# One plain pair of weight tiles instead of two at the start of the second feed-forward block

## The chip, the cores and the metric

The kernel runs on one NeuronCore of a Trainium2 chip. The metric is the device time of one execution in microseconds (us), lower is better. TensorE (PE) multiplies, VectorE (DVE) and ScalarE (ACT) do the elementwise work, GpSimd (POOL) a few small steps, and SyncE (SP) issues the loads. Each of them works through its own instructions in the order in which they stand.

## The reference

One encoder layer on 512 rows of 1024 features: a feed-forward block, a mixer (convolution and a two-way mLSTM), and a second feed-forward block, each between two norms and added to the residual. What the change touches is the feed-forward block:

```python
def rmsnorm(x, g):
    y = x32 * lax.rsqrt(jnp.mean(x32 * x32, axis=-1, keepdims=True) + EPS)
    return (y * g.astype(jnp.float32)).astype(x.dtype)

def swiglu(x, w_in, w_out):
    gate, up = jnp.split(x @ w_in, 2, axis=-1)
    return (jax.nn.silu(gate) * up) @ w_out
...
h = swiglu(rmsnorm(x, norm_ffn2_pre[l]), w_ffn2_in[l], w_ffn2_out[l])
x = x + FFN_RESIDUAL_SCALE * rmsnorm(h, norm_ffn2_post[l])
```

`w_ffn2_in` is 1024 x 5632 (2816 gate columns, then 2816 up columns) and `w_ffn2_out` 2816 x 1024.

## The kernel before, in words

**Precision.** Every float32 operand of a large matmul is split into a high and a low part (`split`: a copy on ACT makes the high part, a subtraction on DVE the low one, L220 and L221), and three matmuls (high x high, high x low, low x high) stand for one.

**The input product of a feed-forward block** (`ffn`). The 2816 gate and up columns are 22 pairs of 128-column weight tiles. The 512 rows are four row tiles of 128. They are handled as two row halves of 256: half 0 is row tiles 0 and 1, half 1 is row tiles 2 and 3. The 1024 features are two halves as well, so that the input is four blocks.

- *The plain way* (`plain`, L361 to L370): a weight tile against one row half is 8 k-blocks x 3 = 24 matmuls of 256 columns. A pair over both halves is 96. The first loop (L373) does row half 0 of all its weight tiles, the second (L377) does row half 1.
- *The seven products* (L398 to L419): gate and up over the two feature halves make a 2x2 block matrix of weights, the input is a 2x2 block matrix too, and seven products of 12 matmuls with added and subtracted blocks replace the eight. A pair is 84 matmuls. `w_pair` makes the weight combinations on DVE and ACT, and the pair's results are put together on DVE and ACT (L403 to L417): `x` is a PSUM tile into which products 1, 6, 7 and 4 accumulate, and it is copied out after product 1 (L403) and after product 6 (L409).
- *Combinations of the input* (`combine_x`, L272 to L293): products 5, 6, 7 and 4 need four combined blocks `t1`, `t2`, `t3`, `t4`, four subtractions (L279) and four splits, which need all four row tiles.

**Why there are plain pairs.** Row tile 3 of the second block comes last: the mixer's output product (L911) ends with it, then `post_norm` (L310) and `pre_norm` (L295) work on it with ACT, DVE and POOL in turn (sum of squares L241, a power on POOL L234, scaling L322, sum of squares, power, scaling L300), then `flip_q` (L261) transposes it on PE (L265), splits it into row half 1, and copies it for `combine_x` (L270). While that goes on, PE does row half 0 of the plain pairs. The dictionary `between` says ahead of which part of which weight tile the transposes of row tile 3 are written: `(3, 2)` is before the low-part matmuls of the fourth weight tile.

**Order.** Instructions are written in program order and a list scheduler of the framework then places them on the engines; what it made is shown below in rows of the built program. Weights come through four raw buffers (`rawp`); `w_get` splits a given number of tiles ahead.

Of the kernel before, what the change touches and what calls it, by code (L numbers as in the profile page):

```python
# [20 lines left out]
KD = D // P  # L21
# [8 lines left out]
WARM = 24  # L30
WARM2 = 4
ON_POOL = (0, 1)
PLAIN = 2


@with_exitstack
def encoder_kernel(ctx: ExitStack, tc: tile.TileContext, a: dict, out: bass.AP):
# [22 lines left out]
    def ps():  # L60
        return psum.tile([P, 512], F32, tag="ps", name=nm("ps"))
# [13 lines left out]
    def blk(i, n=P):  # L75
        return slice(i * n, (i + 1) * n)

    def ch(v):
        return v.rearrange("p (c t) -> p c t", t=P)


    w1i, w1o = a["w_ffn1_in"][0], a["w_ffn1_out"][0]
# [5 lines left out]
    def cols(w, c0):  # L88
        return w[:, c0:c0 + P].rearrange("(k p) f -> p k f", p=P), KD

    def rows(w, r0):
        return w[r0:r0 + P, :], 1

    def one(v):
        return [v[0]], v[1]

    stream = []
    for w_in, w_out in ((w1i, w1o), (w2i, w2o)):
        if w_in is w2i:
            stream += [cols(wm, c) for c in (Q0, Q0 + P, K0, K0 + P)]  # L100
            stream += [cols(wm, O0 + i * P) for i in range(4)]
            stream += [cols(wm, CG)]
            stream += [(wm[blk(i, 2 * P), V0:V0 + 512].rearrange("(k p) f -> p k f", p=P), 2) for i in range(4)]
            for i in range(4):
                stream += [cols(wm, c + i * P) for c in ((CG, HC, BG) if i else (HC, BG))]
            stream += [rows(wo, k * P) for k in MIXK[:5]]
        for j in range(NF):
            pair = [cols(w_in, j * P), cols(w_in, DFF + j * P)]
            stream += pair if j < PLAIN else [([v[0] for v in pair], KD)]
        stream += [rows(w_out, k * P) for k in range(NF)]  # L110
    stream = [v if isinstance(v[0], list) else one(v) for v in stream]
    loaded, ready = [], []
# [67 lines left out]
    def w_get(ahead=2):  # L180
        w_split(max(0, 1 + ahead - len(ready)))
        return ready.pop(0)
# [78 lines left out]
    def flip_q(tb, xs, xq, halves=(0, 1)):  # L261
        for b in halves:
            pt = ps()
            for k in range(4):
                nc.tensor.transpose(out=pt[:, blk(k)], in_=xs[:, blk(4 * b + k)], identity=ident)  # L265
            hi, lo = xq_hl(xq, (b, tb // 2))
            split(hi[:, :, blk(tb % 2)], lo[:, :, blk(tb % 2)], ch(pt))
            if b not in xq["f"]:
                xq["f"][b] = bigt()
            nc.scalar.copy(xq["f"][b][:, :, blk(tb)], ch(pt))  # L270
# [39 lines left out]
    def post_norm(tb, acc, g, mul, after=None):  # L310
        t = [t2() for _ in range(2)]

        def weigh(i):
            nc.vector.tensor_tensor(out=t[i], in0=acc[i], in1=g[:, blk(i, 512)], op=ALU.mult)

        s0 = sumsq(acc[0])
        weigh(0)
        r = rstd([s0, sumsq(acc[1])], D, mul)
        weigh(1)
        for i in range(2):  # L320
            h = blk(i, 512)
            nc.vector.scalar_tensor_tensor(out=x_t[tb][:, h], in0=t[i], scalar=r, in1=x_t[tb][:, h], op0=ALU.mult, op1=ALU.add)  # L322
            if after:
                after(tb, h)
# [22 lines left out]
                nc.tensor.matmul(o, ww[:, k, :], x[xx][:, k, :], start=first and n == 0, stop=n == 11, skip_group_check=True)  # L347
                n += 1

    def ffn(xq, between, finish, mid=None, within=None):  # L350

        h = [bigt() for _ in range((NF + 3) // 4)]

        def act(j, pg, pu):
            sg = t2()
            nc.scalar.activation(sg, pg, AF.Silu)
            nc.vector.tensor_tensor(out=h[j // 4][:, j % 4, 0:512], in0=pu, in1=sg, op=ALU.mult)

        def plain(o, w, th, hooks=None, i=None):  # L361
            hi, lo = w
            n = 0
            for ww, xx in ((hi, 0), (hi, 1), (lo, 0)):
                if hooks and (i, n // KD) in hooks:
                    hooks[i, n // KD]()
                for k in range(KD):
                    nc.tensor.matmul(  # L368
                        o, ww[:, k, :], xq_hl(xq, (k // 4, th))[xx][:, k % 4, :], start=n == 0, stop=n == 3 * KD - 1)
                    n += 1  # L370

        ws, pts = [], []
        for i in range(2 * PLAIN):  # L373
            ws.append(w_get(min(2, 3 - i) if i < 3 else 1))
            pts.append(ps())
            plain(pts[i][:, 0:256], ws[i], 0, between, i)
        for i in range(2 * PLAIN):  # L377
            plain(pts[i][:, 256:512], ws[i], 1)
            if i == 0:
                combine_x(xq)  # L380
            if i % 2:
                act(i // 2, pts[i - 1], pts[i])

        h0, h1 = slice(0, 256), slice(256, 512)
        right = {1: (0, 0), 2: (1, 0), 3: (1, 1), 4: "t4", 5: "t1", 6: "t2", 7: "t3"}

        def product(n, w, o, first):
            mm_part(o[:, h0], w[n], xq_hl(xq, right[n]), first)  # L390

        def last(j, w, x, c, u):
            product(4, w, x, False)
            hj = h[j // 4][:, j % 4, :]
            nc.vector.tensor_tensor(out=hj[:, h0], in0=x[:, h0], in1=c[:, h0], op=ALU.mult)

        pending = None
        for j in range(PLAIN, NF):  # L398
            w = w_get(1 if j < NF - 1 else 2)
            x, y, z = ps(), ps(), ps()  # L400
            a_, u, c = t2(), t2(), t2()
            product(1, w, x, True)
            nc.scalar.copy(a_[:, h0], x[:, h0])  # L403
            product(5, w, y, True)
            nc.scalar.copy(u[:, h0], y[:, h0])
            if pending:
                last(*pending)
            product(6, w, x, False)
            nc.scalar.copy(a_[:, h1], x[:, h0])  # L409
            product(3, w, y, False)  # L410
            nc.vector.tensor_tensor(out=c[:, h1], in0=y[:, h0], in1=a_[:, h1], op=ALU.add)
            product(2, w, z, True)
            nc.vector.tensor_tensor(out=c[:, h0], in0=z[:, h0], in1=a_[:, h0], op=ALU.add)
            nc.scalar.activation(c, c, AF.Silu)
            product(7, w, x, False)
            nc.vector.tensor_tensor(out=u[:, h1], in0=x[:, h0], in1=u[:, h0], op=ALU.add)
            nc.vector.tensor_tensor(out=h[j // 4][:, j % 4, h1], in0=u[:, h1], in1=c[:, h1], op=ALU.mult)  # L417
            pending = (j, w, x, c, u)
        last(*pending)  # L419

        acc = [[ps(), ps()] for _ in range(NT)]
        hs = None
        ks = {}

        def mm_out(tb, half, k, hT, w):
            for hh, ww in ((0, 0), (0, 1), (1, 0)):
                nc.tensor.matmul(  # L427
                    acc[tb][half], hT[hh][:, blk(tb)], w[ww][:, blk(half, 512)],
                    start=(k == 0 and hh == 0 and ww == 0), stop=(k == NF - 1 and hh == 1),
                )  # L430

        for k in range(NF):
            if k % 2 == 0:
                hs = bigt(F32R)
            hT = (hs[:, 2 * (k % 2), 0:512], hs[:, 2 * (k % 2) + 1, 0:512])
            split(hT[0], hT[1], h[k // 4][:, k % 4, 0:512])
            ks[k] = (hT, w_get(2 if k < NF - TAIL else min(2, NF - 1 - k)))
            if k == 12 and mid:
                mid()
            if k < NF - TAIL:  # L440
                for tb in range(NT):
                    for half in range(2):
                        mm_out(tb, half, k, *ks[k])
        for tb in range(NT):
            todo = [(half, k) for half in range(2) for k in range(NF - TAIL, NF)]
            if tb == NT - 1 and mid:
                todo.sort(key=lambda v: v[1])
            for n, (half, k) in enumerate(todo):
                if n == 4 and within:
                    within(tb)  # L450
                mm_out(tb, half, k, *ks[k])
            finish(tb, acc[tb])


    xT1 = new_xq()
    xs = [pre_norm(tb, g_pre) for tb in range(2)]
# [7 lines left out]
    st1 = {}  # L464

    def rest1(tb):
        st1[tb] = pre_norm(tb, g_pre)
# [63 lines left out]
        if tb >= 2:  # L531
            flip(tb - 2, st[tb - 2], st["xT"])

    ffn(xT1, {(1, 0): lambda: rest1(2), (1, 1): lambda: rest1(3), (2, 0): lambda: flip_q(2, st1[2], xT1), (2, 2): lambda: flip_q(3, st1[3], xT1)}, finish1, wgates, within1)
    xT = st["xT"]


# [363 lines left out]
    xT3 = new_xq()  # L901
    xs = {}
    for tb in range(NT):
        acc = [ps(), ps()]
# [14 lines left out]
    g_post3 = gain("norm_ffn2_post")  # L919
# [1 line left out]
    def store(tb, h):  # L921
        nc.sync.dma_start(out[0, blk(tb), h], x_t[tb][:, h])

    ffn(xT3, {(3, 2): lambda: flip_q(3, xs[3], xT3)}, lambda tb, acc: post_norm(tb, acc, g_post3, 4.0, store))


_INS = [
# [26 lines left out]
```

## Time and profile before

| | us |
|---|---|
| three runs | 934.29 (median), 932.46, 934.36 |
| the profiled execution: time | 933.59 |
| the profiled execution: span from first to last instruction | 931.9 |
| PE busy | 920.1 (99%) |
| DVE busy | 633.5 (68%) |
| ACT busy | 417.7 (45%) |

The page also shows the mean granted TensorE clock, 0.996 of full speed. Times in the views are us from the start of the span. The difference of 1.7 between time and span lies around the instructions.

The second block starts at about 581 us. Its input product lasts to about 813 us and its output product to about 926 us.

### The profile page before, as it was taken

How to read it: one execution, taken by the hardware profiler on the slowest of the kernel's cores; microseconds unless marked ns; L12 is line 12 of the kernel's file. 1: busy time of each engine (PE TensorE's matmuls, PEld its weight loads, DVE VectorE, ACT ScalarE, POOL GpSimd, SP SyncE). 2: the span in 40 equal slices, each digit the busy share in tenths (PEclk: the TensorE clock that was granted, in tenths of full speed). 3: DMA queues.
4: the chain of work that ended last, by engine and by line, in shares of the span. 5: the costliest groups of instructions: out<-in, count | busy, mean ns of one | idle time of the engine just before them, and what ended most of it. 6: DMA issues, size and time to landing. Idle time of an engine off the chain costs nothing.

```text
span 931.9 us, 14877 instructions
## 1 busy us (share of the span) xinstructions
PE 920.1 (99%) x6075; PEld 834.9 (90%) x6075; DVE 633.5 (68%) x1028; ACT 417.7 (45%) x685; POOL 39.2 (4%) x64
## 2 busy tenths in 40 slices
PE   7999999999999999999999999999999999999997
PEld 6999999999888889987888888999999999888885
DVE  5989988888822248496767736888888888932223
ACT  6655554556611126452324425645545545721111
POOL 3000000000200001000011000000000000000000
PEclk9999999999999999999999999999999999999999
DMA  8434343344333313231422501323343343443202
GB/s 249 139 91 119 108 128 100 98 129 126 104 133 95 104 52 113 67 93 46 128 76 69 158 24 37 99 73 110 107 121 92 108 120 92 158 136 91 67 9 82
DMA packets 125101, 94.35 MB, mean 101 GB/s; under 512 B 4053, under 2 KB 114665, under 8 KB 125033
## 3 DMA queue, kind: packets, MB, share of 16 engines
q1 hardware_dynamic: 125032, 93.41, 33.7%
q8 instruction: 47, 0.77, 0.3%
q14 instruction: 22, 0.17, 0.1%
HBM read 91.30 MB, written 2.10 MB: 100 GB/s over the span
## 4 chain that ended last, share of the span: by engine, by line
PE 97%; issue 1%; DMA 1%; DVE 1%; ACT 0%; SPq 0%; DVEq 0%; POOLq 0%; POOL 0%; ACTq 0%
PE ps L347 42%; PE ps L427 26%; PE ps L338 13%; PE ps L911 5%; PE ps L368 4%; PE ps L765 2%; PE ps L265 1%; PE ps L832 1%; PE ps L838 1%; DMA gb<-in_norm_ffn_pre_dram 1%; PE ps L801 0%; PE ps L307 0%; PE ps L784 0%; PE ps L806 0%; PE ps L869 0%
## 5 line engine op out<-in xcount | busy, mean ns | idle before, releaser
L221 DVE TENSOR_TENSOR wlo<-raw,whi 128x1024 fp32r<-128x1024 f32 x199 | 241.3, 1220 | 143.3 <-ACT whi L220 137.9
L220 ACT CAST whi<-raw 128x1024 fp32r<-128x1024 f32 x201 | 206.2, 1050 | 222.9 <-PE ps L427 124.2
L347 PE MATMUL ps<-big,whi 128*128 128x256 f32 x1920 | 264.4, 280 | 0.0
L347 PEld LDWEIGHTS ps<-big,whi 128*128 128x128 f32 x1920 | 243.1, 188 | 0.4
L427 PE MATMUL ps<-whi,big 128*128 128x512 f32 x704 | 221.6, 395 | 0.0
L427 PEld LDWEIGHTS ps<-whi,big 128*128 128x128 f32 x704 | 132.2, 188 | 31.1
L347 PE MATMUL ps<-big,wlo 128*128 128x256 f32 x960 | 150.9, 280 | 0.0
L427 PE MATMUL ps<-wlo,big 128*128 128x512 f32 x352 | 139.0, 395 | 0.0
L347 PEld LDWEIGHTS ps<-big,wlo 128*128 128x128 f32 x960 | 129.1, 188 | 0.0
L427 PEld LDWEIGHTS ps<-wlo,big 128*128 128x128 f32 x352 | 66.1, 188 | 15.3
L338 PE MATMUL ps<-big,whi 128*128 128x512 f32 (+1 forms) x384 | 79.8, 358 | 0.0
L338 PEld LDWEIGHTS ps<-big,whi 128*128 128x128 f32 x384 | 63.4, 188 | 11.0 <-issue 0.2
L347 PE MATMUL ps<-big,ws 128*128 128x256 f32 x480 | 65.2, 280 | 0.0
L347 PEld LDWEIGHTS ps<-big,ws 128*128 128x128 f32 x480 | 60.3, 188 | 0.0
L409 ACT COPY t<-ps 128x256 f32<-128x256 f32 x40 | 14.9, 372 | 73.3 <-PE ps L347 73.2
L338 PE MATMUL ps<-big,wlo 128*128 128x512 f32 (+1 forms) x192 | 41.2, 356 | 0.0
L241 ACT ACTIVATE junk<-ps 128x512 bf16<-128x512 f32 x24 | 14.4, 598 | 57.0 <-PE ps L427 26.8
L338 PEld LDWEIGHTS ps<-big,wlo 128*128 128x128 f32 x192 | 32.2, 188 | 5.4
L234 POOL TENSOR_TENSOR rs<-rs,nhalf 128x1 f32<-128x1 f32 x24 | 13.6, 566 | 528.7 <-DVE rs L231 528.7
L368 PE MATMUL ps<-big,whi 128*128 128x256 f32 x256 | 33.5, 283 | 0.1
L221 DVE TENSOR_TENSOR big<-big,big 128x512 fp32r<-128x512 f32 (+1 forms) x48 | 33.0, 731 | 0.7 <-ACT big L220 0.7
L368 PEld LDWEIGHTS ps<-big,whi 128*128 128x128 f32 x256 | 31.6, 190 | 0.4 <-ACT big L220 0.3
(183 smaller groups left out, 937.0 us busy)
## 6 DMA issues: line engine op xcount, KB each, us to landing
raw<-in_w_ffn_in_dram SPq DMA_DIRECT2D x88, 512.0 KB, 4.6
raw<-in_w_ffn_out_dram SPq DMA_DIRECT2D x44, 512.0 KB, 3.6
raw<-in_w_mix_in_dram SPq DMA_DIRECT2D x24, 512.0 KB, 3.9
raw<-in_w_mix_out_dram SPq DMA_DIRECT2D x8, 512.0 KB, 3.6
out_dram<-x SPq DMA_DIRECT2D x8, 256.0 KB, 2.0
x<-in_x_dram SPq DMA_DIRECT2D x4, 256.0 KB, 4.3
x<-in_x_dram SPq DMA_DIRECT2D x2, 512.0 KB
gb<-in_norm_ffn_post_dram SPq DMA_DIRECT2D x2, 512.0 KB, 4.0
```

The costliest lines, as they stand in the source:

```text
L220: nc.scalar.copy(out=hi, in_=src)
L221: eng.tensor_tensor(out=lo, in0=src, in1=f32(hi), op=ALU.subtract)
L234: nc.gpsimd.tensor_tensor(out=r[:, 0:w], in0=acc, in1=nhalf[:, 0:w], op=ALU.pow)
L241: nc.scalar.activation(junk[:, 0:src.shape[1]], src, AF.Square, accum_out=s)
L265: nc.tensor.transpose(out=pt[:, blk(k)], in_=xs[:, blk(4 * b + k)], identity=ident)
L338: nc.tensor.matmul(o, ww[:, k, :], xk(xT, xx, k, sl), start=n == 0, stop=n == 3 * KD - 1)
L347: nc.tensor.matmul(o, ww[:, k, :], x[xx][:, k, :], start=first and n == 0, stop=n == 11, skip_group_check=True)
L368: nc.tensor.matmul(o, ww[:, k, :], xq_hl(xq, (k // 4, th))[xx][:, k % 4, :], start=n == 0, stop=n == 3 * KD - 1)
L409: nc.scalar.copy(a_[:, h1], x[:, h0])
L427: nc.tensor.matmul(acc[tb][half], hT[hh][:, blk(tb)], w[ww][:, blk(half, 512)], start=(k == 0 and hh == 0 and ww == 0), stop=(k == NF - 1 ...
L765: nc.tensor.matmul(pv_, xk(xT, xx, k, blk(tb)), ww[:, k % 2, :], start=n == 0, stop=n == 3 * KD - 1)
L911: nc.tensor.matmul(acc[half], yy[yi][:, k % 4, blk(tb)], wmo[k][wi][:, blk(half, 512)], start=(n == 0 and yi == 0 and wi == 0), stop=(n == ...
```

## The change

The number of plain pairs becomes a parameter of `ffn`: 2 for the first block as before, 1 for the second. The stream of weight loads follows it, the prefetch expression takes the number in, and the transposes of row tile 3 are now written before the low-part matmuls of the second weight tile, `(1, 2)`, which is the last one there is. In the second block the second pair (j = 1) is thus computed by the seven products.

```diff
-PLAIN = 2
...
-            stream += pair if j < PLAIN else [([v[0] for v in pair], KD)]
+            stream += pair if j < (2 if w_in is w1i else 1) else [([v[0] for v in pair], KD)]
...
-    def ffn(xq, between, finish, mid=None, within=None):
+    def ffn(xq, between, finish, PLAIN, mid=None, within=None):
...
-            ws.append(w_get(min(2, 3 - i) if i < 3 else 1))
+            ws.append(w_get(min(2, 2 * PLAIN - 1 - i) if i < 2 * PLAIN - 1 else 1))
...
-    ffn(xT3, {(3, 2): lambda: flip_q(3, xs[3], xT3)}, lambda tb, acc: post_norm(tb, acc, g_post3, 4.0, store))
+    ffn(xT3, {(1, 2): lambda: flip_q(3, xs[3], xT3)}, lambda tb, acc: post_norm(tb, acc, g_post3, 4.0, store), 1)
```

Line numbers after the change are one lower: L367 for L368, L346 for L347, and so on. Three places in the built programs follow. Up to the second block the five engines' rows are the same in both.

**Place A, PE, the end of row half 0 of the plain pairs.** `t_841` is row tile 3 after `pre_norm`; `big_5529` and `big_5539` hold row half 0, `big_5723` and `big_5732` row half 1. Before:

```order
L368 MATMUL ps_5902<-big_5539,whi_5824 128x256 x4
L265 MATMUL ps_5919<-ident,t_841_5758 128x128 x4
L368 MATMUL ps_5902<-big_5529,wlo_5825 128x256 x2
L265 MATMUL ps_5927<-ident,t_841_5758 128x128 x4
L368 MATMUL ps_5902<-big_5529,wlo_5825 128x256 x2
L368 MATMUL ps_5902<-big_5539,wlo_5825 128x256 x4
L347 MATMUL ps_6087<-big_5529,whi_5885 128x256 x8
L347 MATMUL ps_6087<-big_5529,wlo_5886 128x256 x4
L368 MATMUL ps_5797<-big_5723,whi_5781 128x256 x4
```

After:

```order
L367 MATMUL ps_5840<-big_5529,wlo_5788 128x256 x4
L367 MATMUL ps_5840<-big_5539,wlo_5788 128x256 x4
L264 MATMUL ps_5857<-ident,t_841_5758 128x128 x4
L264 MATMUL ps_5865<-ident,t_841_5758 128x128 x4
L346 MATMUL ps_5974<-big_5529,whi_5823 128x256 x8
L346 MATMUL ps_5974<-big_5529,wlo_5824 128x256 x4
L367 MATMUL ps_5791<-big_5723,whi_5781 128x256 x4
L367 MATMUL ps_5840<-big_5723,whi_5787 128x256 x4
```

Between the last L911 and the first L265 on `t_841` PE has 88 matmuls before and 48 after; product 1 of the first seven-product pair (L347, now L346) follows the transposes in both.

**Place B, PE, products 6, 2, 3 and 7 of the first seven-product pair.** `ps_6087` before and `ps_5974` after are its PSUM tile `x`; `big_5975` and `big_5913` hold `t2`, `big_5978` and `big_5916` `t3`. Before:

```order
L347 MATMUL ps_6087<-big_5975,whi_5894 128x256 x8
L347 MATMUL ps_6087<-big_5975,wlo_5895 128x256 x4
L347 MATMUL ps_6089<-big_5539,whi_5885 128x256 x8
L347 MATMUL ps_6089<-big_5539,wlo_5886 128x256 x4
L347 MATMUL ps_6088<-big_5732,whi_5894 128x256 x8
L347 MATMUL ps_6088<-big_5732,wlo_5895 128x256 x4
L347 MATMUL ps_6087<-big_5978,whi_5898 128x256 x8
```

After:

```order
L346 MATMUL ps_5975<-big_5732,whi_5832 128x256 x8
L346 MATMUL ps_5975<-big_5732,wlo_5833 128x256 x4
L346 MATMUL ps_5974<-big_5913,whi_5832 128x256 x4
L346 MATMUL ps_5974<-big_5913,wlo_5833 128x256 x4
L346 MATMUL ps_5974<-big_5916,whi_5836 128x256 x8
```

Before, 24 matmuls of two other products stand between the end of product 6 and product 7 into the same PSUM tile; after, none. From the end of row half 1 to the row with `wlo_5833` into `ps_5974` there are 76 matmuls of the seven-product pairs on PE after the change.

**Place C, DVE, around the first sums of squares of row tile 3** (`rs_5751` comes from them; L221 rows with `wlo` are weight splits). Before:

```order
L314 TENSOR_TENSOR t_834_5742<-ps_5674,gb_5397 128x512
L229 TENSOR_SCALAR rs_5749<-ss_5744 128x1
L221 TENSOR_TENSOR wlo_5788<-raw_5785,whi_5787 128x1024
L221 TENSOR_TENSOR wlo_5794<-raw_5791,whi_5793 128x1024
L221 TENSOR_TENSOR wlo_5825<-raw_5822,whi_5824 128x1024
L221 TENSOR_TENSOR wlo_5886<-raw_5878,whi_5885 128x1024
L221 TENSOR_TENSOR big_5723<-ps_5718,big_5723 128x4x128
L221 TENSOR_TENSOR big_5732<-ps_5727,big_5732 128x4x128
L231 SCALAR_TENSOR_TENSOR rs_5751<-ss_5747,rs_5749 128x1
```

After:

```order
L313 TENSOR_TENSOR t_834_5742<-ps_5674,gb_5397 128x512
L228 TENSOR_SCALAR rs_5749<-ss_5744 128x1
L220 TENSOR_TENSOR wlo_5788<-raw_5785,whi_5787 128x1024
L220 TENSOR_TENSOR wlo_5824<-raw_5816,whi_5823 128x1024
L220 TENSOR_TENSOR big_5723<-ps_5718,big_5723 128x4x128
L220 TENSOR_TENSOR big_5732<-ps_5727,big_5732 128x4x128
L230 SCALAR_TENSOR_TENSOR rs_5751<-ss_5747,rs_5749 128x1
```

Two weight splits fewer stand ahead; from L231 to L300 of row tile 3 the order is the same in both.

## Rows read from the trace of the kernel before

**Rows 1.** Page: busy time by engine; then the shares of the chain that ended last.

```profile
PE 920.1 (99%) x6075; PEld 834.9 (90%) x6075; DVE 633.5 (68%) x1028; ACT 417.7 (45%) x685; POOL 39.2 (4%) x64
PE 97%; issue 1%; DMA 1%; DVE 1%; ACT 0%; SPq 0%; DVEq 0%; POOLq 0%; POOL 0%; ACTq 0%
```

**Rows 2.** That chain in order of time, 581 to 800 us: start, length, what.

```profile
581.44 10.34 PE ps L368 x88
591.79 0.44 PE ps L265 x4
...
593.61 1.38 PE ps L347 x12
595.00 11.31 PE ps L368 x96
606.30 193.66 PE ps L347 x1644
```

**Rows 3.** Timeline of PE, second block's start: start, length, instruction [idle before <-releaser].

```profile
581.28 2.04 PE L368 MATMUL ps<-big,whi 128*128 128x256 f32 x16
...
586.92 2.04 PE L368 MATMUL ps<-big,whi 128*128 128x256 f32 x16
...
591.62 0.60 PE L265 MATMUL ps<-ident,t 128*128 128x128 f32 x4
...
608.52 0.63 PE L347 MATMUL ps<-big,wlo 128*128 128x256 f32 x4
```

**Rows 4.** Timeline of ACT, same stretch.

```profile
581.54 0.60 ACT L241 ACTIVATE junk<-ps 128x512 bf16<-128x512 f32 x1 [0.82 <-PE ps L911]
582.03 0.19 ACT L241 ACTIVATION_READ_ACCUMULATOR junk<-ps 128x1 f32 x1
...
609.19 0.37 ACT L409 COPY t<-ps 128x256 f32<-128x256 f32 x1 [0.52 <-PE ps L347]
```

**Rows 5.** Timeline of DVE, same stretch.

```profile
576.74 4.63 DVE L221 TENSOR_TENSOR wlo<-raw,whi 128x1024 fp32r<-128x1024 f32 x4 [0.18 <-ACT whi L220]
581.28 1.28 DVE L221 TENSOR_TENSOR big<-ps,big 128x512 fp32r<-128x512 f32 x2
582.48 0.15 DVE L231 SCALAR_TENSOR_TENSOR rs<-ss,rs 128x1 f32<-128x1 f32 x1
...
583.15 0.68 DVE L134 TENSOR_TENSOR t<-raw 128x512 f32<-128x512 f32 x1
583.75 1.41 DVE L322 SCALAR_TENSOR_TENSOR x<-t,rs,x 128x512 f32<-128x512 f32 x2
...
587.06 0.69 DVE L134 TENSOR_TENSOR raw<-raw 128x512 f32<-128x512 f32 x1
588.19 1.42 DVE L300 SCALAR_TENSOR_TENSOR t<-x,rs,gb 128x512 f32<-128x512 f32 x2 [0.44 <-POOL rs L234]
```

**Rows 6.** Timeline of POOL, same stretch.

```profile
582.77 0.55 POOL L234 TENSOR_TENSOR rs<-rs,nhalf 128x1 f32<-128x1 f32 x1 [8.96 <-DVE rs L231]
587.24 0.92 POOL L234 TENSOR_TENSOR rs<-rs,nhalf 128x1 f32<-128x1 f32 x1 [3.91 <-DVE rs L231]
```

**Rows 7.** The chain in order of time, first block's start.

```profile
24.00 0.67 DVE t L300
...
24.80 0.64 PE ps L265 x4
```

**Rows 8.** Timeline of PE, the kernel's start: two waits for a normalized row tile.

```profile
9.91 0.66 PE L265 MATMUL ps<-ident,t 128*128 128x128 f32 x4 [3.27 <-DVE t L300]
...
24.80 1.29 PE L265 MATMUL ps<-ident,t 128*128 128x128 f32 x8 [0.80 <-DVE t L300]
```

**Rows 9.** Windows: busy time and (instructions) by engine; PEclk is the column after POOL.

```profile
10.00:14.00 4.00, 4.00 (x22) 4.00 (x23) 3.35 (x6) 3.25 (x6) 1.69 (x1) 0.57 1.07 363
14.00:16.00 2.00, 1.90 (x16) 1.70 (x15) 1.18 (x2) 2.00 (x4) 1.17 (x2) 1.00 1.12 348
24.00:26.00 2.00, 1.17 (x10) 0.98 (x10) 2.00 (x3) 1.79 (x3) 0.00 (x0) 1.00 1.08 313
640.00:700.00 60.00, 60.00 (x512) 60.00 (x511) 50.33 (x80) 30.53 (x49) 0.00 (x0) 1.00 0.37 107
```

More of the change, by code (lines that the diff above doesn't have):

```diff
@@ L532, in within1 @@
             flip(tb - 2, st[tb - 2], st["xT"])
-    ffn(xT1, {(1, 0): lambda: rest1(2), (1, 1): lambda: rest1(3), (2, 0): lambda: flip_q(2, st1[2], xT1), (2, 2): lambda: flip_q(3, st1[3], xT1)}, finish1, wgates, within1)
+    ffn(xT1, {(1, 0): lambda: rest1(2), (1, 1): lambda: rest1(3), (2, 0): lambda: flip_q(2, st1[2], xT1), (2, 2): lambda: flip_q(3, st1[3], xT1)}, finish1, 2, wgates, within1)
     xT = st["xT"]
```

## Prediction

> **What bounds the kernel now.** The page comes first: PE is busy 99% of the span and holds 97% of the chain that ended last [rows 1]. So a change counts by the matmuls that it takes from PE and by the time that it leaves PE without work. The chain in order of time then shows the place of the change, 581.44 to 606.30: 88 + 2 + 6 matmuls of L368 (the short pieces stand between the transposes) for row half 0 of the four plain weight tiles, 8 transposes, 12 matmuls of L347, and 96 of L368 for row half 1, one behind the other [rows 2]. In this stretch PE waits for nothing. In the seven-product stretch 1644 matmuls take 193.66 us, 0.1178 us each, and the 96 plain ones take 11.31, again 0.1178 [rows 2]: whether PE works in the plain way or by products, its price is the count of matmuls.
>
> The plain matmuls of row half 0 are also a cover. Row tile 3 is normalized while they run, and the timelines of DVE, ACT and POOL show how long that takes: PE's last L911 is done at about 581.4, and the second half of the normalized row tile at 588.19 + 1.42 = 589.61 [rows 4, 5]. Before, its transposes came at 591.62 [rows 3], when it had been ready for two us. What cover is left afterwards decides this change.
>
> **The saving.** A pair costs 96 matmuls in the plain way and 84 by products. Before, the second block has 192 + 20 x 84 = 1872, after it 96 + 21 x 84 = 1860. Twelve fewer, at 0.1178 us: **-1.41 us**. Its cover on the other engines is dealt with below.
>
> **The first wait: transposes of row tile 3.** After the change 48 matmuls stand ahead of them (place A). The first plain matmul starts at 581.28 and the 49th at 586.92 [rows 3], so PE comes to the transposes at 586.92. Each of them is queued in PE ahead of product 1 of the first product pair, of row half 1, of everything that follows, so nothing overtakes. When is row tile 3 ready? The chain behind it starts with PE's last L911, which the change doesn't move: sum of squares at 581.54, read out by 582.03 + 0.19 = 582.22 [rows 4]. The next step, L231, comes at 582.48 since DVE is still at the two row-tile splits until then, and these stood behind four weight splits of 4.63 together, 1.16 each [rows 5]. With two of them gone (place C) L231 can follow at about 582.28, 0.2 earlier. The rest of the chain has the same order as before, so I let it keep its durations: power on POOL, L322, squares, L231, power, L300 at 588.19 [rows 5, 6], first half done after half of 1.42, at about 588.9 (the single one of rows 7 takes 0.67). From there to a transpose on PE the first block shows 24.00 + 0.67 = 24.67 to 24.80, 0.13 [rows 7]. So 588.9 + 0.13 - 0.2 = 588.82, and PE stands still from 586.92 on: **+1.9 us**. Bounds: 1.7, if the hand-over costs nothing, and 2.1, if the 0.2 is not won.
>
> The 0.2 is the doubtful part of it, for POOL has its own say. Its power takes 0.55 at 582.77 and 0.92 at 587.24 [rows 6], the second one while L134 runs on DVE from 587.06 to 587.75 [rows 5]. An earlier L231 puts the first power partly beside the L134 that stood at 583.15. The Trainium skill says in GPSIMD Engine Reference, section Specifications, that GpSimd shares its SBUF interfaces with VectorE and contends with DVE instructions that have two SBUF inputs; the trace agrees as far as these two rows go (0.92 against 0.55), and by that rule the first wait would be nearer to 2.1 than to 1.9.
>
> **The second wait.** The other half of row tile 3 is done 0.7 after the first, at 589.61 + 0.13 - 0.2 = 589.54. Four transposes take 0.44 [rows 2], so they end at 588.82 + 0.44 = 589.26: **+0.28 us**. Bounds 0.2 and 0.3.
>
> **The third wait: product 7 of the first product pair.** It accumulates into the PSUM tile that ACT has to copy out after product 6. Before, 24 matmuls (2.8 us) hide the copy; after, product 7 stands right behind (place B). The price from the same copy before: the last matmul of product 6 starts at 608.52 + 3 x 0.118 = 608.87, the next could at 608.99; the copy runs from 609.19 to 609.56 [rows 3, 4], plus 0.13: 609.69. **+0.65 us**, if ACT is free then (0.6 with a quicker hand-over, zero only if PE gets there late for another reason).
>
> **What the second product pair asks of DVE and ACT.** Between the last row-tile split and the low part of `t2` DVE has seven operations of 1.16 and four of 0.60 (four in 4.63; L134 at 583.15, the next at 583.75) [rows 5], 10.5 us together. The splits ahead of them end at about 593.1 (two weight splits from 589.4 on, then two row-tile splits of 0.6), so `t2` is complete at about 603.6. PE starts row half 1 after the transposes and product 1 at 589.54 + 0.44 + 12 x 0.118 = 591.4, ends it 48 matmuls later at 597.05, and has 76 matmuls ahead of the one that needs that low part: 606.0. Cover 2.4 us, so I put it at nothing. Without this cover PE would wait for as much as DVE is late. In the steady stretch DVE is busy 50.33 of 60 us [rows 9], so it catches up about 0.16 us per us. The weight loads are no wait: the product pair's two raw tiles are now third and fourth in the stream instead of fifth and sixth, and the gain's load, which waits for DVE's L314, has moved ahead of the third product pair's loads, first read more than 10 us later.
>
> **Sum.** -1.41 + 1.9 + 0.28 + 0.65 = +1.42 us. On the profiled execution's 933.59 that is 935.0; the median of the runs is 934.29, 0.7 higher, and I forecast from it: **935.7 us**. By the bounds of the three waits alone it is +0.5 to +1.7.
>
> **Rivals.**
>
> *The saving shows.* If row tile 3 came when PE does, PE would save 1.41 less the third wait: -0.8, 933.5. It turns from loss to gain where the three waits together stay under 1.41, so where row tile 3 is 1.4 us earlier than I reckon. For it: DVE has 2.3 us less ahead of the chain. Against it: the chain hangs on PE's last L911 at both ends, and only 0.26 us of it (582.22 to 582.48) is a wait for DVE's weight work. Even with no wait at all it would be 932.9, 0.15% less.
>
> *TensorE's clock falls.* At the start of the kernel PE idles for 3.27 us ahead of a transpose [rows 8], and in the four us from 10 on the granted clock is 0.57, then 1.00 [rows 9]; the level in between is the half speed of 1.2 GHz. That cost 4 x 0.43 = 1.7 us of full speed. After the idle 0.80 at 24 us it stays at 1.00 [rows 8, 9]. The new idle time of 1.9, and 0.28 soon after, lies between the two, nearer to the one that cost nothing. If the clock falls: +1.4 + 1.7 = +3.1, **937.4**, slower. It decides at any fall longer than a us at half speed. The Trainium skill states in TensorE: Matmul & The Clock Gate, section What's actually happening, that the gate goes back to half rate when TensorE has been idle and that activity releases it; the trace agrees for 3.27 us, and no row shows a gap like the new one.
>
> *DVE becomes the bound for the first product pairs.* The second pair's 12 or so DVE operations now run between the steps that make `t1` to `t4`, and copies on ACT stand close to the matmuls that wait for them. For it: DVE has only 16% to spare. Against it: the cover of 2.4 us. Half a weight split to a whole one late (0.6 to 1.2) would give about +2.2, 936.5.
>
> That the change does nothing is ruled out by place A.
>
> **Chances and range.** The forecast 0.58, the saving 0.12, the clock 0.17, DVE 0.13. About 0.2% (1.9 us) is what a measurement here can tell from no change; the three runs of before differ by as much. The forecast lies 0.15% up, so nearly a quarter of it, 0.13, falls over the line, with 0.16 of the clock's and 0.10 of DVE's: slower 0.39. Faster has the saving's edge and a favourable run, 0.04; the rest, 0.57, is no difference. The range goes from the saving's 933.5 to the clock case's upper end: **933.5 to 937.7**, and what it leaves out are runs beside these cases.
>
> **What would show it.** In the timeline of PE, L264 on row tile 3 with an idle time of 1.7 to 2.1 put down to DVE L299, a second of 0.2 to 0.3, and 0.6 before L346 put down to ACT L408; row half 1's 48 plain matmuls and 1764 of L346. In the timeline of DVE, L230 about 0.2 earlier against PE's last L910. Granted clock 1.00 from 586 to 600. Wrong would be: L299's end before 587; a clock under 1; waits of PE for DVE's `wlo` or combined blocks after 600 us; or a change in the output product, where I expect none.

## The result, and the profile after

The changed kernel takes 937.19 us (median of 6 runs, 936.1 to 938.37) against 934.28 (6 runs, 932.46 to 934.51): ratio 1.0035, 95% interval 1.0025 to 1.0045. It is slower by 2.9 us by the medians. The prediction's line for slower was 0.2%, and it gave "no difference" 0.57 and slower 0.39. The time lies in the predicted range; the forecast, 935.7, was too low by half of the effect.

Whole times also hold what happens before the second block, which starts anywhere between 580.5 and 582.1 us in the profiles below. So I also use the **block length**, from the start of the block's first plain matmul to the start of the kernel's last matmul, both read from the timeline of PE. Before it is 344.09 (925.38 - 581.28), after it is 346.97 (927.89 - 580.92), +2.87; the starts shown are rounded, so a last digit can be one off.

The page after (busy time; shares of the chain that ended last), as in [rows 1]:

```profile
PE 919.1 (98%) x6063; PEld 833.2 (89%) x6063; DVE 637.6 (68%) x1038; ACT 420.5 (45%) x690; POOL 39.3 (4%) x64
PE 92%; DVE 2%; DMA 2%; ACT 1%; issue 1%; SPq 0%; POOL 0%; DVEq 0%; POOLq 0%; ACTq 0%
```

PE has the 12 matmuls fewer that were reckoned (6063 for 6075). But it holds 92% of the chain instead of 97%, and loads (DMA) have 2% of it instead of 1%. Where, the chain in order of time shows, as in [rows 2] (start, length, what):

```profile
587.62 0.76 DVE t L299
588.52 0.64 PE ps L264 x4
589.18 0.63 PE ps L264 x4
589.81 1.41 PE ps L346 x12
591.22 5.66 PE ps L367 x48
596.88 9.91 PE ps L346 x84
607.24 10.30 PE ps L346 x85
...
622.00 4.92 DMA raw<-in_w_ffn_in_dram
627.55 0.69 DVE raw L133
...
632.33 4.73 DMA raw<-in_w_ffn_in_dram
637.69 0.70 DVE raw L133
...
642.22 5.17 DMA raw<-in_w_ffn_in_dram
...
649.70 152.85 PE ps L346 x1296
```

In [rows 2] nothing but PE stands between 581 and 800. Now DVE's L299 stands ahead of the transposes, as forecast, and from 622 to 647 three weight loads are on the chain, which was not. The waits of PE from 575 us on (total, times, longest), then that of DVE for loads from 590 to 815:

```profile
PE ps L264 <- DVE t L299: 1.8, 1, 1.8
PE ps L346 <- DVE t L415: 0.7, 2, 0.5
PE ps L346 <- ACT t L408: 0.5, 1, 0.5
```

```profile
DVE t L133 <- DMA raw<-in_w_ffn_in_dram: 8.5, 6, 2.3
```

Before, PE has no wait in that stretch, and DVE one for a load:

```profile
DVE t L134 <- DMA raw<-in_w_ffn_in_dram: 1.0, 1, 1.0
```

The timelines of PE, ACT, DVE and POOL at the places of [rows 3 to 6]:

```profile
580.92 2.04 PE L367 MATMUL ps<-big,whi 128*128 128x256 f32 x16
...
585.62 1.10 PE L367 MATMUL ps<-big,wlo 128*128 128x256 f32 x8
588.52 1.29 PE L264 MATMUL ps<-ident,t 128*128 128x128 f32 x8 [1.80 <-DVE t L299]
...
606.15 0.63 PE L346 MATMUL ps<-big,wlo 128*128 128x256 f32 x4
607.24 1.21 PE L346 MATMUL ps<-big,whi 128*128 128x256 f32 x8 [0.46 <-ACT t L408]
...
628.12 0.63 PE L346 MATMUL ps<-big,wlo 128*128 128x256 f32 x4
629.23 1.22 PE L346 MATMUL ps<-big,whi 128*128 128x256 f32 x8 [0.47 <-DVE t L415]
```

```profile
581.18 0.60 ACT L240 ACTIVATE junk<-ps 128x512 bf16<-128x512 f32 x1
581.67 0.19 ACT L240 ACTIVATION_READ_ACCUMULATOR junk<-ps 128x1 f32 x1
...
606.82 0.37 ACT L408 COPY t<-ps 128x256 f32<-128x256 f32 x1 [3.51 <-PE ps L346]
```

```profile
581.90 0.16 DVE L230 SCALAR_TENSOR_TENSOR rs<-ss,rs 128x1 f32<-128x1 f32 x1 [0.71 <-ACT junk L240]
...
587.62 1.41 DVE L299 SCALAR_TENSOR_TENSOR t<-x,rs,gb 128x512 f32<-128x512 f32 x2 [0.44 <-POOL rs L233]
...
620.76 2.35 DVE L220 TENSOR_TENSOR wlo<-raw,whi 128x1024 fp32r<-128x1024 f32 x2
...
626.94 0.69 DVE L133 TENSOR_TENSOR t<-raw 128x512 f32<-128x512 f32 x1 [2.29 <-DMA raw<-in_w_ffn_in_dram]
627.55 0.68 DVE L133 TENSOR_TENSOR raw<-raw 128x512 f32<-128x512 f32 x1
628.15 0.69 DVE L133 TENSOR_TENSOR raw<-raw,raw 128x512 f32<-128x512 f32 x1
628.75 0.42 DVE L415 TENSOR_TENSOR t<-ps,t 128x256 f32<-128x256 f32 x1
```

```profile
582.20 0.55 POOL L233 TENSOR_TENSOR rs<-rs,nhalf 128x1 f32<-128x1 f32 x1 [8.75 <-DVE rs L230]
586.67 0.92 POOL L233 TENSOR_TENSOR rs<-rs,nhalf 128x1 f32<-128x1 f32 x1 [3.91 <-DVE rs L230]
```

*The first three waits* are there. From the start of the 48th plain matmul (586.44) to the first transpose (588.52) it is 2.08, less the 0.12 that a matmul takes: 1.96 us lost. The third is 0.74 - 0.12 = 0.62 by the same reading, and the matmul after each wait comes 0.1 later than usual as well.

*The loads* are the new thing. Two weight splits run from 620.76 to 623.1; the first ends at about 622.0 and frees its raw buffer. The load into this buffer has landed at 626.92, and DVE stands 2.29 us at L133, which reads it. Behind L133 in DVE's row stands L415, which takes product 7's result out of the PSUM tile into which PE wants to accumulate product 4, so PE waits 0.47 us by this view and 0.75 - 0.12 = 0.63 by its starts. The same comes again near 639 (the starts are 0.23 apart, so 0.11) and at 649 (0.47 apart, so 0.35). With the 0.1 behind each, the three cost 1.4 us.

### The profile page after: what moved, and what is told of

It is laid out like the page before. It is cut to its first block, busy times and chain, and to the rows that moved or that the text cites. A ratio compares the mean times of both kernels' runs of the same rounds, so it can differ in the third digit from the quotient of the medians.

```text
span 934.4 us, 14881 instructions
## 1 busy us (share of the span) xinstructions
PE 919.1 (98%) x6063; PEld 833.2 (89%) x6063; DVE 637.6 (68%) x1038; ACT 420.5 (45%) x690; POOL 39.3 (4%) x64
## 4 chain that ended last, share of the span: by engine, by line
PE 92%; DVE 2%; DMA 2%; ACT 1%; issue 1%; SPq 0%; POOL 0%; DVEq 0%; POOLq 0%; ACTq 0%
PE ps L346 40%; PE ps L426 26%; PE ps L337 13%; PE ps L910 5%; PE ps L764 2%; PE ps L367 2%; DMA raw<-in_w_ffn_in_dram 2%; DVE wlo L220 1%; PE ps L831 1%; PE ps L837 1%; PE ps L264 1%; DMA gb<-in_norm_ffn_pre_dram 1%; PE ps L800 0%; PE ps L306 0%; DVE raw L133 0%
## 5 line engine op out<-in xcount | busy, mean ns | idle before, releaser
L346 PE MATMUL ps<-big,whi 128*128 128x256 f32 x1968 | 271.0, 280 | 1.1 <-DVE t L415 0.7
L346 PEld LDWEIGHTS ps<-big,whi 128*128 128x128 f32 x1968 | 249.0, 188 | 2.2 <-DVE t L415 1.2
L346 PE MATMUL ps<-big,wlo 128*128 128x256 f32 x984 | 154.0, 280 | 0.0
L346 PEld LDWEIGHTS ps<-big,wlo 128*128 128x128 f32 x984 | 132.1, 188 | 0.0
L337 PEld LDWEIGHTS ps<-big,whi 128*128 128x128 f32 x384 | 63.3, 188 | 11.0 <-issue 0.2
L346 PE MATMUL ps<-big,ws 128*128 128x256 f32 x492 | 68.4, 280 | 0.0
L346 PEld LDWEIGHTS ps<-big,ws 128*128 128x128 f32 x492 | 62.4, 188 | 0.0
L133 DVE TENSOR_TENSOR t<-raw 128x512 f32<-128x512 f32 x41 | 28.1, 685 | 14.2 <-DMA raw<-in_w_ffn_in_dram 14.2
L337 PEld LDWEIGHTS ps<-big,wlo 128*128 128x128 f32 x192 | 32.2, 188 | 5.4
L413 ACT ACTIVATE t<-t 128x512 f32<-128x512 f32 x41 | 25.9, 633 | 23.1 <-DVE t L410 22.3
```

The source lines that it names most:

```text
L133: nc.vector.tensor_tensor(out=o, in0=a_, in1=b_, op=op)
L337: nc.tensor.matmul(o, ww[:, k, :], xk(xT, xx, k, sl), start=n == 0, stop=n == 3 * KD - 1)
```

## The experiments

Three theories. **A**: the three early waits add up to the loss, with the 12 matmuls saved. **L**: PE's waits from 620 us on come from late weight loads (rival **V**: DVE simply has too much work there). **C**: in some executions TensorE's clock falls after the first wait. Ratios are to runs of the kernel before on the same chip, with 95% intervals.

| run | kernel | median us (before) | ratio | block length of its profile, against 344.09 |
|---|---|---|---|---|
| e1 | changed, six raw buffers | 935.99 (933.85) | 1.0024 [1.0015, 1.0033] | +3.03 |
| e2 | before, six raw buffers | 934.00 (933.85) | 1.0003 [0.9994, 1.0011] | 0.00 |
| e3 | changed, no wait for row tile 3 | 935.67 (933.85) | 1.0019 [1.0011, 1.0028] | +1.23 |
| e4 | e1, products 1 and 2 first | 933.67 (933.85) | 0.9998 [0.9989, 1.0007] | -0.12 |
| e5 | changed, again | 938.05 (933.85) | 1.0044 [1.0030, 1.0058] | +2.70 |
| e6 | changed, PE kept busy | 936.89 (933.85) | 1.0035 [1.0023, 1.0048] | +2.70 |
| e7 | e1, PE kept busy | 935.65 (933.85) | 1.0018 [1.0009, 1.0026] | +1.44 |
| e8 | before, 12 matmuls fewer | 932.27 (933.85) | 0.9983 [0.9974, 0.9992] | -1.62 |
| e9, e10, e11 | changed, one execution each | 936.53, 938.19, 938.44 | | +3.08, +4.46, +4.48 |
| e12 | changed, products 1 and 2 first | 934.39 (933.82) | 1.0010 [1.0001, 1.0019] | +0.79 |

**e1 and e2: two more raw buffers.**

```diff
+    pairs2 = [n for n, v in enumerate(stream) if len(v[0]) == 2][-(NF - 1):]
+    spare = set(pairs2[3::3])
...
-                    raw = rawp.tile([P, 1024], F32, tag="raw", name=nm("raw"))
+                    raw = t4(F32) if late else rawp.tile([P, 1024], F32, tag="raw", name=nm("raw"))
```

> The changed kernel, with two more raw buffers for the second block's product pairs: every third pair of weight tiles, from the fourth product pair on, is loaded into the two buffers of the pool t4p, which are free there; nothing else is changed. Theory L (loads): PE's waits at 628 and 649 us come from weight loads that are issued only when one of four raw buffers comes free and that VectorE then waits for, with its own later steps queued behind. Then these waits go, the three early ones (1.96, 0.25 and 0.62 us) stay, and the time is 1.2 to 1.6 us under the changed kernel's: about +1.4 us on the kernel before, ratio 1.0015. Theory V (VectorE has too much work for the first product pairs, whatever the loads do): the waits stay, +2.9 us, ratio 1.003.

> Control: the kernel before with the same two more buffers (every third product pair from the fourth on). PE has no waits in its second block, so both theories L and V expect no difference: within 0.1% of the kernel before. If it is faster by as much as e1 is against the changed kernel, the buffers help for another reason and e1 tells nothing on the waits.

The control is flat, 1.0003. In e1 PE's waits from 575 us on are these alone:

```profile
PE ps L267 <- DVE t L302: 1.8, 1, 1.8
PE ps L349 <- ACT t L411: 0.5, 1, 0.5
```

All waits of PE after 610 us are gone, and DVE waits for no load between 590 and 815, which decides for L against V: DVE has the same work. But the time came down less than expected, and the block length of its profile not at all. The windows of its profile show why (busy us and instructions of PE first; the granted clock is the third number from the end):

```profile
588.00:589.00 1.00, 0.21 (x2) 0.24 (x3) 1.00 (x2) 1.00 (x2) 0.00 (x0) 1.00 0.00 0
...
590.00:591.00 1.00, 1.00 (x7) 1.00 (x6) 1.00 (x2) 0.46 (x2) 0.00 (x0) 0.50 0.00 0
591.00:592.00 1.00, 1.00 (x6) 1.00 (x6) 1.00 (x2) 1.00 (x2) 0.00 (x0) 0.50 0.12 34
592.00:593.00 1.00, 1.00 (x8) 1.00 (x7) 0.94 (x3) 0.89 (x3) 0.00 (x0) 0.60 1.02 301
593.00:594.00 1.00, 1.00 (x11) 1.00 (x10) 1.00 (x2) 0.40 (x1) 0.00 (x0) 1.00 0.95 265
```

The clock falls to half right behind the first wait. In the first profile of the changed kernel it had not. Theory C comes from here.

**e3: no wait for row tile 3.**

```diff
-    ffn(xT3, {(1, 2): lambda: flip_q(3, xs[3], xT3)}, lambda tb, acc: post_norm(tb, acc, g_post3, 4.0, store), 1)
+    ffn(xT3, {(1, 2): lambda: flip_q(3, xs[2], xT3)}, lambda tb, acc: post_norm(tb, acc, g_post3, 4.0, store), 1)
```

> The changed kernel, but the transposes ahead of row half 1 read row tile 2 instead of row tile 3 (row tile 3's values are left out of the second block's product, so the output isn't the reference's). The first two waits, 1.96 and 0.25 us, are gone. If waits add up (theory A): 2.2 us less than the changed kernel, +0.7 us on the kernel before, ratio 1.0007. If the loads and VectorE's combinations are what PE catches up with (theory L): most of the 2.2 comes back as more and longer waits of PE for ScalarE's copies and VectorE's combining steps between 594 and 650 us, and the time is only 0.3 to 1.2 us under the changed kernel's, +1.7 to +2.6 us, ratio about 1.002.

Between the two: by block length 1.6 us are won on the changed kernel's +2.87, not 2.2, and by its ratio it is still 1.8 us over the kernel before, in theory L's range. Of the 1.6, 0.4 lies in the output product, which is that much shorter here; no run shows why. In the input product 1.3 are won. With PE earlier, the load waits grow; the row of 629.23 shown above becomes

```profile
628.35 1.21 PE L346 MATMUL ps<-big,whi 128*128 128x256 f32 x8 [0.89 <-DVE t L415]
```

0.89 instead of 0.47. So the waits do not simply add up: part of an early wait is time in which the late loads catch up.

**e4 and e12: products 1 and 2 of the first product pair ahead of the transposes**, with six raw buffers and with four (`start` and `start2` issue the two products, `late` the transposes of row tile 3).

```diff
+        if late:
+            start(PLAIN)
+            start2(PLAIN)
+            late()
...
+            if j in ahead:
+                (w, x, z), y = ahead[j], ps()
...
+    ffn(xT3, {}, lambda tb, acc: post_norm(tb, acc, g_post3, 4.0, store), 1, late=lambda: flip_q(3, xs[3], xT3))
```

> e1's kernel, with products 1 and 2 of the first product pair (24 matmuls that need row half 0 alone) ahead of the transposes of row tile 3. They cover 2.8 us, so the first wait goes; product 1 no longer covers the split behind the transposes, so a wait of about 0.6 us appears there and one of 0.5 to 0.8 for the first combined block; with product 2 done early VectorE's and ScalarE's steps shift, and the third wait may go. Theory A and L: -1.41 + 1.4 to 1.9 us of waits, so 0 to +0.5 us on the kernel before, ratio 1.000 to 1.0005. If something beyond waits of PE costs time in the changed kernel (a rival that no wait shows), it stays above +1 us, ratio over 1.001.

> The changed kernel with products 1 and 2 of the first product pair ahead of row tile 3's transposes, as in e4, but with the four raw buffers. The first and third wait are covered, PE never idles for over a us, so the clock can't fall; the loads are late again. Theory L: waits of 0.4 to 0.7 us for VectorE's combining steps near 628 and 639 us come back, about 1 us in all, and it is 0.7 to 1.2 us slower than e4, ratio on the kernel before 1.0005 to 1.0012. If the six buffers matter only together with the early waits, it equals e4, ratio 1.000.

Both medians are as expected. With 24 matmuls as a cover the first wait is gone; one of 0.52 for the first combined block appears, as the timeline of e4 shows:

```profile
590.80 1.38 PE L267 MATMUL ps<-ident,t 128*128 128x128 f32 x8
592.13 3.88 PE L370 MATMUL ps<-big,whi 128*128 128x256 f32 x28
...
598.88 0.74 PE L349 MATMUL ps<-big,ws 128*128 128x256 f32 x4 [0.52 <-ACT big L222]
```

e4 is as fast as the kernel before and no faster (0.9998): what 12 matmuls save, the rest of the waits takes. In the input product alone it is 0.3 us behind: from the block's first plain matmul to the first matmul of the output product it takes 800.89 - 582.08 = 218.81, before 799.80 - 581.28 = 218.52. Its output product is 0.4 shorter, as in e3. e12, with four raw buffers, is 0.9 us longer in its block than e4 (+0.79 against -0.12; 0.8 in the input product), and DVE waits 5.7 us for loads between 590 and 660 in it: the price of the loads without the first and third wait. Its runs go from 933.64 to 936.41, wider than those of the kernel before; its profile is the shortest of them, and what the long ones hold is not shown.

**e5, e6 and e7: keeping PE busy through the first wait.** e6 and e7 put 16 matmuls of operands that are there already into a PSUM tile that nobody reads; PE's other matmuls keep their order.

```diff
+            pd = ps()
+            for n in range(16):
+                nc.tensor.matmul(
+                    pd[:, 0:256], ws[1][0][:, n % 8, :], xq_hl(xq, (n % 8 // 4, 0))[0][:, n % 4, :], start=True, stop=True)
+            late()
```

> The changed kernel itself, to see how its runs spread and to stand beside e6 and e7 on one chip. Theory C (clock): in some executions TensorE's clock falls to half after the wait for row tile 3, as in the profile of e1 (matmuls 0.213 us apart, granted clock 0.50 from 590 to 592), in others not, as in the first profile of the changed kernel. Then its runs spread over more than the 2 us of the kernel before, with a median near +2.9 us, ratio 1.003. If the clock has nothing to do with it, the spread is like that of the kernel before.

> The changed kernel with 16 more matmuls (1.9 us, of operands that are there already, into a PSUM tile that nobody reads) between row half 0 and the transposes of row tile 3, so that PE works while it would wait. All else is in the same order. Theory C: the clock can't fall, so the long runs go; what stays is the waits and the loads, as in the first profile: +2.4 to +2.6 us, ratio 1.0027, and a spread no wider than that of the kernel before; the gain on e5 is small since a later PE waits less for the loads. Rival (only waits count): equal to e5 within its spread.

> e1's kernel (two more raw buffers) with e6's 16 matmuls. Theory C and L: neither clock nor loads are left, only the three early waits: -1.41 + 1.96 + 0.25 + 0.7 = +1.4 to +1.5 us, ratio 1.0015, its runs within 1.5 us of each other, and about 0.6 us under e1's median. Rival (the clock doesn't matter): equal to e1, +2.1 us, with runs spread over 3 us as e1's.

e7 is the clean one: no late loads, no fall of the clock in its profile, and a block of +1.44 us. PE has one wait left from 575 us on:

```profile
PE ps L349 <- ACT t L417: 0.5, 1, 0.5
```

Its 16 matmuls take the place of the first wait: from the first of them (587.08) to the first transpose (589.04) it is 1.96, as long as that wait. So it shows the forecast's sum (+1.42), with the first term put in by hand. Its median is 0.34 under e1's (measured on another chip, where the kernel before has the same median), less than the 0.6 expected. Its runs go from 934.40 to 936.14, 1.7 and not 1.5 apart, while e1's reach 937.74. e6 and e7 differ in the raw buffers alone, and by 2.70 - 1.44 = 1.26 us in their blocks: the price of the loads. e5's runs go from 936.41 to 938.46, with a median of +4.2, not +2.9. e6 missed its expectation: its profile has the full clock and +2.70, but its five runs go from 935.96 to 939.20, wider than I allowed, and they overlap e5's, so by their times e6 doesn't decide between theory C and its rival. Its two longest runs were not profiled; their mean granted clocks, 0.992 and 0.994, are below the 0.995 to 0.997 of the other three, but where in the span the clock was lower is not on record.

**e8: what 12 matmuls are worth.**

```diff
-            product(3, w, y, False)
+            if j != 8 or xq is not xT3_[0]:
+                product(3, w, y, False)
```

> The kernel before without product 3 of the seventh product pair of the second block (12 matmuls left out, so those columns are not the reference's). It prices the saving alone: if PE's matmul count is the price, -1.41 us, ratio 0.9985. If VectorE or the loads set the pace of the product stretch (theory V), less than 0.5 us is won.

0.9983, and -1.62 in the block against -1.41 expected (-1.49 in the input product, the rest in the output product): matmuls taken from PE where nothing waits come off the time in full.

**e9 to e11: three more executions of the changed kernel, each with its profile.**

> The changed kernel, one profiled execution. Theory C: executions of 937 us and more are those in which the granted clock falls to 0.5 for about three us after one of PE's waits in the second block; those near 936 show 1.00 throughout after 20 us. If a profile of 937.5 or more shows the full clock, theory C is wrong and longer load waits (over 2.3 us on VectorE) should show in its place.

> The same kernel and question as in the first look, a second execution: near 936 us with the clock at 1.00, or 937.5 and more with a stretch at 0.5.

> The same kernel and question as in the first look, a third execution: near 936 us with the clock at 1.00, or 937.5 and more with a stretch at 0.5.

The window from 590 to 592 us in e9 (936.53 us), e10 (938.19) and e11 (938.44), in this order:

```profile
590.00:592.00 2.00, 2.00 (x20) 2.00 (x19) 2.00 (x3) 1.54 (x2) 0.00 (x0) 1.00 0.12 30
```

```profile
590.00:592.00 2.00, 2.00 (x11) 2.00 (x10) 2.00 (x3) 1.46 (x3) 0.00 (x0) 0.50 0.07 18
```

```profile
590.00:592.00 2.00, 2.00 (x11) 2.00 (x11) 2.00 (x3) 1.61 (x3) 0.00 (x0) 0.52 0.01 2
```

Theory C holds for these three: the two long executions are those with the clock at half (11 matmuls in 2 us, 20 in the other), after the same wait of 1.8 us. The fall costs 4.47 - 2.88 = 1.6 us, the difference of the block lengths of e10 and e11 to the mean of the three profiles at full clock (the first, e5, e9). For runs without a profile it is not shown. Their mean granted clocks don't settle it: 0.996 in the three profiled executions at full clock and 0.994 to 0.995 in the three with the fall (e1, e10, e11), but 0.996 also in e5's runs of 937.58 and 938.05, and 0.998 in the run of 937.29 among the first six.

## Why the prediction was right in part, and where it failed

*The saving, -1.41: right.* The count is 6063 for 6075, and e8 prices 12 matmuls at 1.5 to 1.6 us.

*The first wait, +1.9: right,* 1.96, and the 0.2 that it was to win on DVE was won: L230 follows the sum of squares at once (581.90, 0.98 after PE's first plain matmul, against 1.20 before [rows 3, 5]). POOL's power, of which I feared contention with L133, kept its 0.55 there, and the second one its 0.92. *The second, +0.28:* the transposes are 0.66 apart in the chain instead of 0.44, so 0.2. *The third, +0.65:* 0.62, and 0.1 for the matmul behind it. (The prediction's own times, 608.99 and 609.69, give 0.70 and not 0.65.)

*The sum, +1.42: right for what it held.* e7 shows it, with 16 matmuls in place of the first wait, +1.44. That the time lies in the range is luck in part: by the bounds of the three waits it would be +0.5 to +1.7, and +2.9 is in the range only because its upper end was taken from the clock's case.

*What failed is "The weight loads are no wait"*, put at nothing. It is worth 1.3 us by e6 against e7, and 1.3 to 1.6 us by the changed kernel at full clock (+2.70 to +3.08) against e7; e12 against e4 gives 0.9 without the first and third wait. I looked at when the first loads are issued and not at the ring of four buffers behind them: a split frees a buffer, the next load has landed in it 4.7 to 5.2 us later, and DVE, in its fixed order, waits for it with PE's next release behind. Why the kernel before is spared is worked out and not tested by a run of its own: its second plain pair gives this ring a lead. A plain pair is 96 matmuls, 11.3 us of PE, and asks of DVE two weight splits of 1.16 [rows 5] and one shorter step, while a product pair takes PE 9.9 and DVE in the steady stretch 0.84 of that [rows 9]. In the trace of before DVE waits for a load once in this stretch, 1.0 us, and PE never.

*The rival of DVE* had PE wait for the combined blocks near 606. There PE shows no wait, so the cover of 2.4 us held. The waits came at 629 to 650, for DVE's L415, and had another cause: the rival asked whether DVE has time, and e1 shows that with more buffers the same DVE work fits.

*The rival of the clock* was given 0.17. Of six profiles with this wait (the first, e1, e5, e9, e10, e11) the clock fell in three, which is what the prediction named as a sign of being wrong (a clock under 1). Its price, 1.7 us by [rows 9], was 1.6. So the runs of the changed kernel are likely a mixture: block lengths of about +2.9 at full clock and about +4.5 when it falls, and the median of the first six runs, +2.9, and of e5's five, +4.2, within these. By its time the result is nearest to this rival's 937.4, but for a sum of two causes: loads in every profile with four raw buffers, the clock in half of the six. The Trainium skill's rule that I cited (TensorE: Matmul & The Clock Gate, section What's actually happening) agrees with e1, e10 and e11 in that idle time brings the half rate. How much idle time does it, the measurement decides: 1.8 us was enough in three profiles and not in three.

Left open: the longest runs of e6 and e12. In the profiles of neither does PE idle for more than 0.3 us at the place of the first wait, so something besides a fall of the clock behind that wait lengthens some runs.

## What to carry to other kernels

Work that looks like waste on the bound engine can give a lead to three other things at once: to a dependent chain, to the buffers of a load stream, and to the clock. Before taking 1.4 us from it, read from the trace how long each of them needs, and count the ring behind each buffer (split, load, wait, release), not only the first loads. Useful work that needs nothing late (here products 1 and 2) covers such a wait without the waste, yet it only brought this change back to level.

## What the runs showed of the hardware that was not expected

After an idle time of TensorE of 1.8 us by the profile (1.96 by the starts), amid work that is otherwise dense, the granted clock fell to 0.50 in three of six profiles and stayed at 1.00 in three. Five of the six are of the changed kernel itself, with one order of instructions and the same wait, and in two of these five it fell (the sixth is e1); a fall cost 1.6 us. The same kernel thus has executions 1.6 us apart. Nor did a longer idle time always bring the fall: at its start e12 idles for 2.33 us ahead of a transpose, and the clock stays at 1.00 in the four us from 10 on, where the kernel before has 0.57 after 3.27 us [rows 8, 9]:

```profile
8.98 0.66 PE L264 MATMUL ps<-ident,t 128*128 128x128 f32 x4 [2.33 <-DVE t L299]
```

```profile
10.00:14.00 4.00, 2.55 (x18) 1.83 (x17) 2.90 (x6) 3.50 (x7) 2.12 (x1) 1.00 1.05 383
```

After each of the waits at 607, 629, 639 and 649 us the second matmul started 0.22 us after the first instead of the usual 0.118, so a wait costs about 0.1 us more than the idle time that the view of the waits gives.
